# Attention products of few keys made 128 rows deep with zero weights, and three VectorE steps of the first layer's chunks put at the priority of the weight splits

## The chip, the cores and the metric

The kernel runs on one core of one Trainium2 chip. The metric is the device time in microseconds (us), from the first to the last instruction with what lies around them; the median of the runs is compared. Before the change the median of three runs is 934.2 us (933.96 to 939.34). A core has a matrix engine (TensorE, PE in the profile, with its weight loads as PEld), VectorE (DVE), ScalarE (ACT), GpSimd (POOL) and SyncE (SP), which issues most of the DMAs.

## The reference

One inference step of a two-layer decoder, for a prompt of 512 tokens and 8 samples of 4 tokens each (544 columns in all), model width 1024, float32. Cut to what matters here:

```python
def ssd_scan(xdt, adt, bm, cm, init):            # first layer: state-space mixer, chunks of 128 tokens
    seg = exp(where(tri, a_cs[..., :, None] - a_cs[..., None, :], -inf))
    cb = einsum("bctgn,bcsgn->bcgts", Cc, Bc)
    m = einsum("bcgts,bgjcts->bcgjts", cb, seg)                  # masked products times decays
    y_diag = einsum("bcgjts,bcsgjp->bctgjp", m, X)               # X = x * dt
    chunk_states = einsum("bctgn,bgjct,bctgjp->cbgjpn", Bc, decay_in, X)
    ...
def dilated_attn_prompt(q, k, v, bvec, dil, nw): # second layer: keys at distances 0, d, .., nw*d
    p = exp(scores - lse[..., None])
    o = einsum("brnhqk,brnkhd->brnqhd", p, vb)
def dilated_attn_sample(q, kc, vc, bvec, dil, nw, n_old):  # 1024 cached rows and the 4 new ones
    scores = einsum("bthd,btjhd->bthj", q, kg) * (q.shape[-1] ** -0.5) + bvec.T[None, None]
    o = einsum("bthj,btjhd->bthd", p, vg)
```

There are three dilation groups (windows 128, 512, 2048 with distances 1, 4, 16), 8 key heads of width 128, 32 state-space heads in 4 groups. The projections before and after, the norms, the convolution and the shared keys and values complete the step.

## The kernel before, in words

Float32 weights and activations of the big projections are split into a high and a low part (`whi`, `wlo`, `nh`, `nl`, ...), and three products replace one. `split_w` (lines 200 to 211) does this for a weight tile: ScalarE copies the high part (L205), VectorE subtracts it (L206). `load_w` (L213) fetches a tile and puts the split at high priority (`tc.high_priority()`), so that the scheduler places it ahead of waiting work on its engine. The order of the instructions of each engine is otherwise the scheduler's, from the order of the program and its own estimates.

The first layer (about 60 to 350 us of the span) is a filler of input projections (`filler_a`: products into `pa` and `pb`, then the convolution `co` on ScalarE and VectorE, L635 to L646, or the gate `uz`, L681), into which the units of the state-space mixer are woven: for each of 4 groups four chunks of 128 tokens (`ssm_chunk`) and two quads of samples (`ssm_quad`). A chunk on TensorE: transposes and a product into the PSUM tiles `cbp` and `xp`; VectorE then makes `xdt` and `xdd` (`xp` scaled by two vectors, L743 and L745), `cbm` (the masked product, L747) and `m` (L748); on later turns TensorE multiplies into `csp`, `yo` and `yd`. A quad does the like, with `cbs`, `xdt`, `xdd` at high priority already, and updates the states with four products `up` (L855 to L862). These PSUM tiles share five buffers (`pss`), so a product into a new tile can wait until VectorE or ScalarE has read an old one. `xdt` and `xdd` of chunks and quads share three SBUF buffers.

The second layer's attention (about 590 to 870 us) is woven the same way: the filler (`pair_filler`, then `out_proj`) makes the query and gate projections, and 48 units `attend(h, n)` (head h, query block n of 128) and `sample(h, q)` run beside them, each in stages. In `attend` the scores of the two wider groups stand in w = 32 (n + 1) columns for each class of positions modulo 4; the probabilities are transposed (`ptp`), copied by ScalarE into `pt` (L1403, L1404), and multiplied with the values (`pv`): blocks of 128 keys with 128 columns, then for each of the 4 classes a product of w key rows and 32 columns into its own 32 partitions (L1410). In `sample` the transposed probabilities `wt` of 640 cached keys are multiplied with the cached values `vc` into `so`, 5 blocks of 128 keys and 32 columns for each of 4 samples, and then the 4 new keys: a product of 4 key rows (`vn`, L1486). A float32 product appears in the trace as two matmuls with two weight loads. The cached keys `kc` and values `vc` (640 KB a load, two buffers each) come through SP's queue, as do the weights.

The lines that set these products:

```python
        pt = wk.tile([128, 3, 128], F32, name="pt", bufs=2)                       # L1402
        nc.scalar.copy(pt[0:w, 2, :], tp[0:w, 2, :])                              # L1404
        for r in range(4):                                                        # L1410
            mm(pv[32 * r:32 * r + 32, :], pt[0:w, 2, 32 * r:32 * r + 32], vr[0:w, r, :], ...)
...
                    mm(so[rows, :], wt[0:TS, 5, rows], vn[:, j, :], start=False, stop=True, ...)   # L1486
```

## Time and profile before

| | before |
|---|---|
| median of 3 runs | 934.2 us (933.96 to 939.34) |
| profiled execution, its own time | 930.12 us |
| its span | 928.3 us, 21878 instructions |
| VectorE busy | 683.7 us (74%), 1435 instructions |
| ScalarE busy | 489.6 us (53%) |
| GpSimd busy | 163.9 us (18%) |
| DMA | 168.48 MB, mean 182 GB/s |

The profile is of one execution, taken by the hardware. A group in it is named by line, engine, operation and tiles: `L146 PE MATMUL so<-vn,wt 4*32` is a matmul issued at line 146 (the helper `mm`, which all products share) that writes `so` from `vn` and `wt`, with 4 rows and 32 columns of the array in use. A row of the timeline gives start, duration, engine, line, operation and count, and in square brackets how long the engine had stood idle and what ended that. Neighbouring instructions are merged, and matmuls overlap, so a busy TensorE can still lose time between products.

### The profile page before, as it was taken

To read this page: it belongs to the slowest core of one execution; us is meant where nothing else is said; L and a number is where in the kernel's file an instruction comes from. 1 tells how busy PE (TensorE), PEld (TensorE's weight loads), DVE (VectorE), ACT (ScalarE), POOL (GpSimd) and SP (SyncE) were. 2 spreads that over 40 slices of the span, in tenths; PEclk is the share of its full clock that TensorE was granted. 3 is DMA by queue.
4 is the path that set the end of the run, shared out by engine and by line. 5 is a ranking of instruction groups with operands and counts; after the bars stand their busy time and mean duration, and the time that the engine had idled before them with its cause. 6 is when DMAs were issued, how large, how long until landed. Compare 5 with 4: busy or idle time off the path is not lost.

```text
span 928.3 us, 21878 instructions
## 1 busy us (share of the span) xinstructions
PE 912.0 (98%) x8671; PEld 842.9 (91%) x8671; DVE 683.7 (74%) x1435; ACT 489.6 (53%) x1140; POOL 163.9 (18%) x206
## 2 busy tenths in 40 slices
PE   8999999999999999999999999999999999999997
PEld 8989888988788889999999999988888888888997
DVE  6998899989799799555598346866677766777732
ACT  6678655755665655322255213555555555557642
POOL 2030344533433533111011000000000000000021
PEclk9999999999999999999999999999999999999999
DMA  8224365365357432546286555767867877784511
GB/s 296 92 74 158 97 212 188 122 200 159 127 171 233 138 132 96 159 137 209 84 285 204 190 177 181 255 208 250 279 192 250 265 228 255 258 267 144 191 49 49
DMA packets 80573, 168.48 MB, mean 182 GB/s; under 512 B 19990, under 2 KB 37736, under 8 KB 79960
## 3 DMA queue, kind: packets, MB, share of 16 engines
q1 hardware_dynamic: 73784, 154.60, 50.8%
q10 hardware_dynamic: 5616, 9.75, 2.8%
q0 software_dynamic: 1072, 2.74, 1.2%
q8 instruction: 68, 1.11, 0.5%
q14 instruction: 33, 0.27, 0.1%
HBM read 141.14 MB, written 25.93 MB: 180 GB/s over the span
## 4 chain that ended last, share of the span: by engine, by line
PE 82%; DVE 10%; ACT 2%; DMA 2%; issue 2%; POOL 0%; SPq 0%; ACTq 0%; POOLq 0%; DVEq 0%
PE pa L146 33%; PE pb L146 28%; PE sp L146 3%; PE so L146 3%; PE pv L146 2%; PE s L146 2%; DVE wlo L206 2%; DVE co L641 1%; PE yd L146 1%; DVE vl L874 1%; DMA m<-aed 1%; PE w L149 1%; PE ptp L149 1%; PE csp L146 1%; PE xp L149 1%
## 5 line engine op out<-in xcount | busy, mean ns | idle before, releaser
L205 ACT ACTIVATE whi<-wraw 128x1024 fp32r<-128x1024 f32 x69 | 72.9, 1056 | 95.7 <-PE pb L146 53.0
L206 DVE TENSOR_TENSOR wlo<-wraw,whi 128x1024 fp32r<-128x1024 f32 x69 | 88.8, 1287 | 46.9 <-ACT whi L205 46.4
L146 PE MATMUL pa<-bq,whi 128*128 128x272 f32 x512 | 103.1, 296 | 0.0
L146 PE MATMUL pb<-nl,whi 128*128 128x288 f32 x280 | 83.6, 298 | 0.0
L146 PE MATMUL pb<-nh,wlo 128*128 128x288 f32 x280 | 83.1, 297 | 0.0
L146 PE MATMUL pb<-nh,whi 128*128 128x288 f32 x280 | 83.0, 296 | 0.0
L146 PEld LDWEIGHTS pa<-bq,whi 128*128 128x128 f32 x512 | 81.2, 189 | 0.9
L146 PE MATMUL pa<-nh,whi 128*128 128x256 f32 x280 | 80.0, 286 | 0.0
L146 PE MATMUL pa<-nl,whi 128*128 128x256 f32 x280 | 79.7, 285 | 0.0
L146 PE MATMUL pa<-nh,wlo 128*128 128x256 f32 x280 | 79.1, 282 | 0.0
L146 PE MATMUL pb<-bq,whi 128*128 128x272 f32 x384 | 77.2, 296 | 1.2 <-DVE kv L1225 0.8
L146 PE MATMUL pa<-bq,wlo 128*128 128x272 f32 x256 | 74.2, 290 | 0.0
L641 DVE SCALAR_TENSOR_TENSOR co<-cb,cvp,co 128x568 f32<-128x568 f32 x72 | 65.4, 911 | 1.3 <-ACT co L639 0.7
L146 PEld LDWEIGHTS pb<-bq,whi 128*128 128x128 f32 x384 | 60.8, 189 | 2.5 <-DVE kv L1225 1.0
L1284 ACT ACTIVATE whi<-wraw 128x512 fp32r<-128x512 f32 x64 | 40.1, 627 | 36.4 <-PE pb L146 16.6
L146 PEld LDWEIGHTS pb<-nl,whi 128*128 128x128 f32 x280 | 52.5, 188 | 4.4 <-issue 4.4
L146 PE MATMUL pb<-bq,wlo 128*128 128x272 f32 x192 | 55.4, 289 | 0.0
L146 PEld LDWEIGHTS pb<-nh,wlo 128*128 128x128 f32 x280 | 52.7, 188 | 2.2 <-issue 2.2
L146 PEld LDWEIGHTS pa<-nh,whi 128*128 128x128 f32 x280 | 52.8, 189 | 1.9 <-issue 1.9
L146 PEld LDWEIGHTS pa<-nl,whi 128*128 128x128 f32 x280 | 52.7, 188 | 1.4 <-issue 1.4
L146 PEld LDWEIGHTS pa<-nh,wlo 128*128 128x128 f32 x280 | 52.7, 188 | 0.9 <-issue 0.9
L146 PEld LDWEIGHTS pb<-nh,whi 128*128 128x128 f32 x280 | 52.6, 188 | 0.8 <-issue 0.8
(403 smaller groups left out, 2779.7 us busy)
## 6 DMA issues: line engine op xcount, KB each, us to landing
wraw<-w_in SPq DMA_DIRECT2D x40, 512.0 KB
kc<-ck SPq DMA_DIRECT2D x32, 640.0 KB
vc<-cv SPq DMA_DIRECT2D x32, 640.0 KB
wraw<-wb SPq DMA_DIRECT2D x32, 512.0 KB
s<-s SPq DMA_DIRECT2D x32, 256.0 KB
m<-aed SPq DMA_DIRECT2D x16, 512.0 KB
ssmS<-s ACTq DMA_DIRECT2D x32, 256.0 KB
wraw<-w_out SPq DMA_DIRECT2D x16, 512.0 KB
```

Source lines behind the costliest of these rows:

```text
L146: pin(nc.tensor.matmul(*a, **k))
L149: pin(nc.tensor.transpose(*a))
L205: a = nc.scalar.activation(hi, raw, AF.Copy)
L206: b = lo_eng.tensor_tensor(lo, raw, f32(hi), op=ALU.subtract)
L641: nc.vector.scalar_tensor_tensor(o, cb[:, k:k + n], cvp[:, ti, k:k + 1], o, op0=ALU.mult, op1=ALU.add)
L874: nc.vector.scalar_tensor_tensor(v_l[g][:, i, :], v_t[g][:, i, :], gg, f32(v_h[g][:, i, :]), op0=ALU.mult, op1=ALU.subtract)
L1284: nc.scalar.activation(hi, src[p][j], AF.Copy)
```

## The change

Two edits. In the attention the products of few keys are made 128 rows deep. Four single tiles `ptz[n]`, one for each query block, take the transposed probabilities of the wider groups in their first w rows; their other rows are set to zero once by GpSimd, and the product reads all 128 rows, with all 128 rows of `vr`. `wt` and `vn` of the samples become single tiles allocated once; row 4 and on of `vn` and of `wt[:, 5]` are zeroed once, and the product with the new keys reads 128 rows. `pt` shrinks from three to two blocks. In the first layer `xdt`, `xdd` and `cbm` of a chunk are issued at high priority, as the weight splits are.

```diff
         xdt = wk.tile([128, 8, HP], F32, name="xdt", tag="xd", bufs=3)
-        nc.vector.tensor_tensor(xdt, xph, bc(tok[:, c, 1, hs], HP), op=ALU.mult)
         xdd = wk.tile([128, 8, HP], F32, name="xdd", tag="xd", bufs=3)
-        nc.vector.tensor_tensor(xdd, xph, bc(tok[:, c, 2, hs], HP), op=ALU.mult)
         cbm = wk.tile([128, 128], F32, name="cbm")
-        nc.vector.tensor_tensor(cbm, cbp[:, 0:128], tri, op=ALU.mult)
+        with tc.high_priority():
+            nc.vector.tensor_tensor(xdt, xph, bc(tok[:, c, 1, hs], HP), op=ALU.mult)
+            nc.vector.tensor_tensor(xdd, xph, bc(tok[:, c, 2, hs], HP), op=ALU.mult)
+            nc.vector.tensor_tensor(cbm, cbp[:, 0:128], tri, op=ALU.mult)
...
-    for t_ in qpad + [sbt]:
+
+    ptz = [wk.tile([128, 128], F32, name=f"ptz{i}", bufs=1) for i in range(4)]
+    wt = wk.tile([128, 6, 128], F32, name="wt", bufs=1)
+    vn = wk.tile([128, 4, 128], F32, name="vn", bufs=1)
+    for t_ in qpad + [sbt, vn, wt[:, 5, :]] + ptz:
         nc.gpsimd.memset(t_, 0.0)
...
-        pt = wk.tile([128, 3, 128], F32, name="pt", bufs=2)
+        pt = wk.tile([128, 2, 128], F32, name="pt", bufs=2)
         nc.scalar.copy(pt[:, 0:nk, :], tp[:, 0:nk, :])
-        nc.scalar.copy(pt[0:w, 2, :], tp[0:w, 2, :])
+        nc.scalar.copy(ptz[n][0:w, :], tp[0:w, 2, :])
...
-            mm(pv[32 * r:32 * r + 32, :], pt[0:w, 2, 32 * r:32 * r + 32], vr[0:w, r, :],
+            mm(pv[32 * r:32 * r + 32, :], ptz[n][:, 32 * r:32 * r + 32], vr[:, r, :],
                start=False, stop=True, skip_group_check=True)
...
-        vn = wk.tile([TS, 4, 128], F32, name="vn", bufs=1)
-        dma(vn, dap(vnd, h * 128 + 4 * q * TS * ATH * 128, [[ATH * 128, TS], [TS * ATH * 128, 4], [1, 128]]))
+        dma(vn[0:TS], dap(vnd, h * 128 + 4 * q * TS * ATH * 128, [[ATH * 128, TS], [TS * ATH * 128, 4], [1, 128]]))
...
-        wt = wk.tile([128, 6, 128], F32, name="wt", bufs=1)
...
-                if i < 5:
-                    mm(so[rows, :], wt[:, i, rows], vc[j // 2][:, j % 2, i, :], start=i == 0, stop=False, skip_group_check=True)
-                else:
-                    mm(so[rows, :], wt[0:TS, 5, rows], vn[:, j, :], start=False, stop=True, skip_group_check=True)
+                vals = vc[j // 2][:, j % 2, i, :] if i < 5 else vn[:, j, :]
+                mm(so[rows, :], wt[:, i, rows], vals, start=i == 0, stop=i == 5, skip_group_check=True)
```

TensorE's order of products is the same in both kernels, throughout. VectorE's order moves at about a dozen places of the first layer; ScalarE's, GpSimd's and SP's shift by a few rows there. The first place is VectorE's queue late in the third group's first quad and second chunk, before the change (`st` to `v` finish the chunk, `xr` belongs to the quad; `xdt`, `xdd` and `cbm` are of the next chunk, `wlo` is a weight split):

```order
L761 TENSOR_TENSOR st<-csp,st 128x512
L766 TENSOR_TENSOR ea<-yo,ea 128x512
L220 SCALAR_TENSOR_TENSOR xr<-xdd,csts,xr 128x512
L777 TENSOR_TENSOR v<-yd,ea 128x4x128
L743 TENSOR_TENSOR xdt<-xp,tok 128x512
L206 TENSOR_TENSOR wlo<-wraw,whi 128x1024
L745 TENSOR_TENSOR xdd<-xp,tok 128x512
L747 TENSOR_TENSOR cbm<-cbp,csts 128x128
```

The same place on VectorE after it (line numbers are one higher):

```order
L762 TENSOR_TENSOR st<-csp,st 128x512
L220 SCALAR_TENSOR_TENSOR xr<-xdd,csts,xr 128x512
L767 TENSOR_TENSOR ea<-yo,ea 128x512
L778 TENSOR_TENSOR v<-yd,ea 128x4x128
L746 TENSOR_TENSOR xdt<-xp,tok 128x512
L747 TENSOR_TENSOR xdd<-xp,tok 128x512
L206 TENSOR_TENSOR wlo<-wraw,whi 128x1024
L748 TENSOR_TENSOR cbm<-cbp,csts 128x128
```

`xdd` now stands ahead of the split, `cbm` still behind it, and `xr` ahead of `ea`.

The second place is VectorE's queue some 12 us earlier, in the same quad, before (`co` and `CT` are the convolution, `btr` and `cbs` read the quad's `cbp`):

```order
L641 SCALAR_TENSOR_TENSOR co<-cb,cvp,co 128x568
L828 TENSOR_TENSOR xdt<-xp,tok 128x512
L220 SCALAR_TENSOR_TENSOR btr<-cbp,csts,btr 128x128
L822 TENSOR_TENSOR cbs<-cbp,csts 128x16
L644 SCALAR_TENSOR_TENSOR CT<-cb,co 128x512
```

And after:

```order
L641 SCALAR_TENSOR_TENSOR co<-cb,cvp,co 128x568
L220 SCALAR_TENSOR_TENSOR btr<-cbp,csts,btr 128x128
L823 TENSOR_TENSOR cbs<-cbp,csts 128x16
L829 TENSOR_TENSOR xdt<-xp,tok 128x512
L644 SCALAR_TENSOR_TENSOR CT<-cb,co 128x512
```

`btr` and `cbs` moved ahead of `xdt`.

The third place is the like of the second one group earlier (the second group's first quad), on VectorE before:

```order
L828 TENSOR_TENSOR xdt<-xp,tok 128x512
L220 SCALAR_TENSOR_TENSOR btr<-cbp,csts,btr 128x128
L822 TENSOR_TENSOR cbs<-cbp,csts 128x16
L644 SCALAR_TENSOR_TENSOR CT<-cb,co 128x512
L645 SCALAR_TENSOR_TENSOR CT<-cb,co 128x32
```

And after:

```order
L829 TENSOR_TENSOR xdt<-xp,tok 128x512
L644 SCALAR_TENSOR_TENSOR CT<-cb,co 128x512
L645 SCALAR_TENSOR_TENSOR CT<-cb,co 128x32
L220 SCALAR_TENSOR_TENSOR btr<-cbp,csts,btr 128x128
L823 TENSOR_TENSOR cbs<-cbp,csts 128x16
```

Here `btr` and `cbs` moved behind the two parts of `CT`.

## The prediction

> **What bounds the kernel now.** I read the page first, then the stages, then who waits for whom, and last the timeline of the products that the change touches. The page gives the engines' busy time and the chain that ended last:

> ```profile
> PE 912.0 (98%) x8671; PEld 842.9 (91%) x8671; DVE 683.7 (74%) x1435; ACT 489.6 (53%) x1140; POOL 163.9 (18%) x206
> PE 82%; DVE 10%; ACT 2%; DMA 2%; issue 2%; POOL 0%; SPq 0%; ACTq 0%; POOLq 0%; DVEq 0%
> ```

> The same by stages, with start and end, length, then busy us (and instructions) of PE, PEld, DVE, ACT, POOL, and the DMA share before GB/s:

> ```profile
> 60.00:350.00 290.00, 287.59 (x2366) 257.56 (x2366) 260.94 (x408) 182.13 (x449) 115.80 (x125) 1.00 0.49 160
> 590.00:870.00 280.00, 279.25 (x3511) 245.81 (x3509) 201.38 (x618) 156.13 (x420) 4.59 (x16) 1.00 0.71 236
> ```

> TensorE is never idle for long in either stage. In the first layer all its idle time that another engine ended is this:

> ```profile
> PE up L146 <- DVE xdd L745: 1.6, 1, 1.6
> PE yd L146 <- DVE cbs L822: 0.6, 1, 0.6
> PE xp L149 <- DVE xs L644: 0.2, 1, 0.2
> ```

> So VectorE, though busy for 261 of 290 us, costs TensorE some 2.4 us. In the attention the busy number hides losses, because matmuls overlap. They show in the weight loads. TensorE's row of the products with cached values is first, then the loads of the product with the four new keys and of what follows:

> ```profile
> 605.67 1.30 PE L146 MATMUL so<-vc,wt 128*32 128x128 f32 x40
> 606.90 0.15 PEld L146 LDWEIGHTS so<-vn,wt 4*32 4x32 f32 x8 [0.20 <-issue]
> 607.25 0.16 PEld L146 LDWEIGHTS s<-kc,qpad 128*32 128x32 f32 x8 [0.20 <-PE so L146]
> ```

> The loads stand still for 0.20 us when the rows in use go from 128 to 4, and again when they go back. The same stands around products of 64 rows, not around those of 96 or 128:

> ```profile
> 612.49 0.15 PEld L146 LDWEIGHTS pv<-kv,pt 64*32 64x32 f32 x8
> 612.84 0.16 PEld L146 LDWEIGHTS sp<-kv,qp 128*32 128x32 f32 x8 [0.20 <-issue]
> 618.39 0.13 PEld L146 LDWEIGHTS sp<-kv,qp 128*32 128x32 f32 x4
> 629.28 0.16 PEld L146 LDWEIGHTS pv<-kv,pt 128*32 128x32 f32 x8
> 629.53 0.24 PE L146 MATMUL sp<-kv,qp 128*32 128x64 f32 x4
> 869.95 0.19 PEld L146 LDWEIGHTS pa<-yh,wo 128*128 128x128 f32 x1 [0.20 <-issue]
> ```

> The row at 618.39 follows the 96-row product of block 2 and carries no wait; 629.28 is block 3, already 128 rows, which is what the changed kernel issues everywhere.

> **The attention products, part by part.** The number of products, from the rows of the tiles (two matmuls each, four products a unit):

> ```profile
> L146 PEld LDWEIGHTS so<-vc,wt x640: 106/110/111, 605.7 to 854.3; 128*32 128x32 f32 x160
> L146 PEld LDWEIGHTS so<-vn,wt x128: 101/103/104, 606.9 to 854.6; 4*32 4x32 f32 x128
> L146 PE MATMUL pv<-kv,pt x368: 267/275/377, 600.5 to 869.8; 128*128 128x128 f32 x56, 32*32 32x128 f32 x32, 64*32 64x128 f32 x32, 96*32 96x128 f32 x32
> ```

> Samples: 128 / 8 = 16 units. From the start of `so` to the start of the following product is 607.25 - 605.67 = 1.58 us now. The forty matmuls with `vc` go in ten groups of four; the last starts 1.30 - 0.27 = 1.03 after the first, less 0.02 within its group, so nine steps take 1.01 and one step 0.112. With twelve groups alike, the next product starts twelve steps after the first: 1.34. The gain is 0.24 a unit, 16 x 0.24 = 3.8 us.

> Prompt: eight heads, so eight units of each block. After the wait a load and its matmul start together, so block 1 takes 612.84 - 612.49 = 0.35 from its first narrow product to the next, and block 3 takes 629.53 - 629.28 = 0.25. The gain is 0.10 where the rows are 32 or 64 and a product with 32 columns follows: eight units of block 1 and seven of block 0. The last block 0 is followed by the output projection with 128 columns, which waits anyway (869.95), and blocks 2 and 3 gain nothing. The wait ahead of the narrow products stays, since it is there in block 3 too, where 128 columns give way to 32. 15 x 0.10 = 1.5 us. Together 5.3 us on the engine that sets the end.

> What padding adds: a load of 128 rows takes 110 ns against 103, so 128 x 7 ns = 0.9 us if the loads stood in a row, and nothing if they hide behind products, as those of `vc` do: forty loads of 110 ns within 1.03 us. I take nothing, since block 3 with 128 rows shows the step above already. [...]

> Six more GpSimd memsets stand where these stand now:

> ```profile
> 571.17 0.64 POOL L1178 MEMSET sbt<- 128x644 f32 x1
> 570.99 0.69 DVE L1285 TENSOR_TENSOR wlo<-sums,whi 128x512 fp32r<-128x512 f32 x1 [0.81 <-ACT whi L1284]
> ```

> They write 512 + 5 x 128 = 1152 columns, at 0.64 / 644 each 1.1 us, from 571.8 on. The first narrow product comes at 600, VectorE is not slowed beside a memset (0.69), so I cost them at nothing; without that cover it would be 1.1 us. The rest has one answer: ScalarE's copies, the DMA of `vn`, and the buffers keep their size, places and waits (`vn` and `wt` had one buffer before).

> Now what comes late next. TensorE already waits for cached keys twice:

> ```profile
> PEld s L146 <- DMA kc<-ck: 1.3, 2, 0.7
> ```

> Those loads are issued after the previous `so`, behind others in SP's queue, so where they already end the wait, a faster TensorE only waits longer: in each such stretch one `so` and two `pv` gain 0.24 + 0.20 = 0.44, lost again. 2 x 0.44 = 0.9 us; none lost at best, and all 5.3 at worst if every sample came to wait so. The attention keeps 4.4 us.

> **The first layer.** At the 1.6 us wait, VectorE's and TensorE's rows:

> ```profile
> 249.39 0.67 DVE L743 TENSOR_TENSOR xdt<-xp,tok 128x512 f32<-128x512 f32 x1
> 251.26 1.23 DVE L206 TENSOR_TENSOR wlo<-wraw,whi 128x1024 fp32r<-128x1024 f32 x1 [1.19 <-ACT whi L205]
> 252.40 0.68 DVE L745 TENSOR_TENSOR xdd<-xp,tok 128x512 f32<-128x512 f32 x1
> 253.00 0.28 DVE L747 TENSOR_TENSOR cbm<-cbp,csts 128x128 f32<-128x128 f32 x1
> 253.20 0.18 PEld L146 LDWEIGHTS up<-xr,btr 32*128 32x128 f32 x1 [1.93 <-issue]
> 253.23 0.61 PE L146 MATMUL up<-xr,btr 32*128 32x512 f32 x2 [1.65 <-DVE xdd L745]
> ```

> VectorE stood behind a split that waited for ScalarE, with `xdd` queued behind; TensorE's second `up` needed the buffer that `xdd` frees. Now `xdd` goes first. But the third `up` needs the buffer that `cbm` reads, and `cbm` stays behind the split; it comes 0.60 earlier, by the length of `xdd`. So I take 0.6, with bounds of 0 and 1.9, the whole wait. At the second place of the order:

> ```profile
> 238.62 0.68 DVE L828 TENSOR_TENSOR xdt<-xp,tok 128x512 f32<-128x512 f32 x1
> 239.47 0.16 DVE L822 TENSOR_TENSOR cbs<-cbp,csts 128x16 f32<-128x16 f32 x1
> 239.69 1.09 PE L146 MATMUL yd<-m,xdt 128*64 128x128 f32 x16 [0.57 <-DVE cbs L822]
> ```

> `cbs` goes ahead of `xdt`, some 0.6 earlier, and the 0.57 goes. At the third place it goes the other way:

> ```profile
> 167.65 0.16 DVE L822 TENSOR_TENSOR cbs<-cbp,csts 128x16 f32<-128x16 f32 x1
> 167.73 0.89 DVE L644 SCALAR_TENSOR_TENSOR CT<-cb,co 128x512 f32<-128x512 f32 x1
> 168.62 0.33 PE L146 MATMUL yd<-m,xdt 128*64 128x128 f32 x2
> ```

> `cbs` moves behind `CT` (0.89 and its small part of 0.1) and ends at about 168.8, later than `yd` starts; if that `yd` waits for `cbs` as the other did, it loses 0.2 to 0.4. I take 0.25, bounds 0 and 1. Elsewhere `xdt`, `xdd` and `cbm` overtake convolution steps and, at five places, a split. What waits behind is then 0.6 later each time, and the splits have more room than that:

> ```profile
> 222.75 2.38 DVE L206 TENSOR_TENSOR wlo<-wraw,whi 128x1024 fp32r<-128x1024 f32 x1
> 227.59 0.29 PE L146 MATMUL pa<-nh,wlo 128*128 128x256 f32 x1
> ```

> This one, among the latest, ends 2.5 us before its first use. So nothing is charged there. First layer: 0.6 + 0.57 - 0.25 = 0.9 us gained.

> **The sum.** 4.4 + 0.9 = 5.3 us. The profiled execution took 930.12 us (span 928.3), so it would take 924.8. It lies 4.1 under the median of the runs shown, 934.2, and I carry that distance over: 928.9 us.

> **Rivals.** First, the first layer gives all it can: both waits go whole (1.9 + 0.57), the third place costs nothing, and no key load bites. Then 5.3 + 2.5 = 7.8, 926.4 us. For it: TensorE waits for nothing else there. Against it: `cbm` is still behind the split.

> Second, the cached loads take most of the attention's gain. DMA is busy for 0.71 of the stage, and SP issues them late. If half is lost, 5.3 / 2 = 2.7 is left, with nothing net from the first layer: 931.5 us. Against it: only two of 16 samples waited.

> Third, slower: VectorE's queue is held by a step put forward too early. `cbm` waits for a copy by ScalarE:

> ```profile
> 322.90 0.29 DVE L747 TENSOR_TENSOR cbm<-cbp,csts 128x128 f32<-128x128 f32 x1 [1.46 <-ACT btok L740]
> ```

> Here VectorE stood 1.46 us. The change moves `cbm` forward at six places; behind it queue convolution steps, the splits and the reads that free PSUM, and TensorE waits for these once VectorE is 2.5 us behind. If all six stood 1.46 and TensorE bore it, 8.8 would be lost: 934.2 - 4.4 + 8.8 = 938.6 us. It ends above 934.2 from 4.4 us of such waits on. Against it: at those places ScalarE's copy was done before VectorE came to `cbm`, mostly by over a microsecond, and VectorE waited so only twice in the whole layer.

> Fourth, padded loads no longer slip under running products, so that eight loads in a row cost 8 x 0.11 = 0.88 us where now the narrow group takes 0.35 and the wait ahead of it 0.20. Then 31 units (16 and 15) lose 0.33 each, 10.2 us: 944.4 us. [...]

> Fifth, the waits belong to something else than the rows and stay: 934.2 less 0.9, about 933.3. The missing wait behind 96 rows speaks against it.

> **How the numbers follow.** Chances: forecast 0.55, first rival 0.15, second 0.14, third 0.08, fourth 0.02, fifth 0.04, and 0.02 for a gain beyond all of these. The forecast's own range, with its unknown costs (0 to 0.9 from the key loads, 0 to 1.9 and 0 to 1 from the first layer), is 926.5 to 930.5. Down to the first rival with 1.9 us for the runs' own scatter, and up past the second by 1 us, it holds over 8 in 10: 924.5 to 932.5. A measurement of this kernel can tell about 1% from no change, here below 924.9 or above 943.5. Faster than that needs the first rival and scatter, 0.08; slower needs the third at its worst or the fourth, 0.04; the rest, 0.88, lies within 1%.

> **What would show it.** In the profile after: the loads of `so<-vn` with 128*32 and without a wait, those of `s` behind `so` without one; 0.25 us instead of 0.35 behind `pv` in blocks 0 and 1; longer waits of `s` for `kc`, but at two to four samples only; no wait of `up` for `xdd`, a shorter one for `cbm`; none of `yd` for `cbs` at 239, a small one at 168. The prediction is wrong if TensorE shows new waits in the first layer that add up to over 2 us, if waits for `kc` exceed 2.5 us, or if the 0.20 us waits stand beside 128 rows.

## The result and the profile after

| | before | after |
|---|---|---|
| median of 7 runs, the same rounds | 934.33 us (933.96 to 939.34) | 927.23 us (924.51 to 932.11) |
| ratio, with its 95% interval | | 0.9913 (0.9884 to 0.9941) |
| a second timing, later: 5 runs of after, 23 of before | 933.46 us | 927.1 us, ratio 0.9935 (0.9922 to 0.9948) |
| profiled execution, its own time | 930.12 us | 932.11 us |

The change makes the kernel 6 to 8 us faster, 0.65 to 0.87%, less than the 1% that I counted as telling. The forecast was 928.9 us with a range of 924.5 to 932.5. One thing has to be kept in mind in reading the two profiles: the profiled execution of the changed kernel was the slowest of its seven, and the first one of the kernel before faster than all seven of its timed runs. Side by side they say "2 us slower". Only stage by stage do they say what happened.

First the page's busy times and chain, then the stretches 60 to 350 and 590 to 870 us, of the changed kernel:

```profile
PE 908.9 (98%) x8671; PEld 847.9 (91%) x8671; DVE 687.5 (74%) x1435; ACT 489.9 (53%) x1140; POOL 163.0 (18%) x212
PE 82%; DVE 9%; DMA 4%; ACT 2%; issue 2%; POOL 0%; SPq 0%; POOLq 0%; DVEq 0%; ACTq 0%
```

```profile
60.00:350.00 290.00, 284.75 (x2322) 254.96 (x2321) 259.65 (x399) 179.06 (x446) 114.11 (x125) 0.99 0.48 157
590.00:870.00 280.00, 277.54 (x3548) 252.63 (x3548) 204.58 (x628) 159.06 (x423) 4.59 (x16) 1.00 0.73 243
```

In the 290 us of the first layer TensorE gets through 44 products fewer (2322 for 2366); in the 280 us of the attention through 37 more (3548 for 3511), though it starts late into them. The chain has 4% of waits for transfers where it had 2%. TensorE's order of products is the same in both, so the starts can be compared product by product. From the product that starts at 60.1 us before the change to the one at 360.1, the changed kernel takes 5.6 us longer in this execution; from 360.1 to 572.5 exactly as long; from 572.5 to 873.1, the attention, 3.9 us less.

The loads around the products of few keys, in the changed kernel, a sample and then a prompt block 0:

```profile
611.28 1.03 PEld L146 LDWEIGHTS so<-vc,wt 128*32 128x32 f32 x40 [0.20 <-DMA bt<-bvd]
612.29 0.24 PEld L146 LDWEIGHTS so<-vn,wt 128*32 128x32 f32 x8
612.51 0.24 PEld L146 LDWEIGHTS s<-kc,qpad 128*32 128x32 f32 x8
...
606.52 0.16 PEld L146 LDWEIGHTS pv<-kv,ptz 128*32 128x32 f32 x8
606.66 0.40 PEld L146 LDWEIGHTS sp<-kv,qp 128*32 128x32 f32 x16
```

The waits of 0.20 us ahead of `so<-vn` and of `s` are gone, and that ahead of `sp` behind block 0 (the prediction shows the same rows before the change, for block 1). What TensorE waited for between 60 and 350 us:

```profile
PE xp L149 <- DVE xs L644: 2.1, 1, 2.1
PE up L146 <- DVE cbm L748: 1.4, 1, 1.4
PE yd L146 <- ACT yos L825: 1.2, 1, 1.2
PE pa L146 <- DVE uz L681: 0.5, 1, 0.5
```

The waits for `xdd` and `cbs` that stood there before, 2.2 us, are gone, and 5.2 us of others stand in their place.

### The profile page after: what moved, and what is told of

Read it like the earlier page. It is cut to its first block, busy times and chain, and to the rows that moved or that the text cites. A ratio compares the mean times of both kernels' runs of the same rounds, so it can differ in the third digit from the quotient of the medians.

```text
span 930.2 us, 21888 instructions
## 1 busy us (share of the span) xinstructions
PE 908.9 (98%) x8671; PEld 847.9 (91%) x8671; DVE 687.5 (74%) x1435; ACT 489.9 (53%) x1140; POOL 163.0 (18%) x212
## 4 chain that ended last, share of the span: by engine, by line
PE 82%; DVE 9%; DMA 4%; ACT 2%; issue 2%; POOL 0%; SPq 0%; POOLq 0%; DVEq 0%; ACTq 0%
PE pa L146 33%; PE pb L146 28%; PE sp L146 3%; PE pv L146 2%; PE so L146 2%; PE s L146 2%; DVE wlo L206 2%; DMA kc<-ck 1%; PE yd L146 1%; DMA m<-aed 1%; DVE co L641 1%; PE csp L146 1%; PE w L149 1%; PE ptp L149 1%; PE xp L149 1%
## 5 line engine op out<-in xcount | busy, mean ns | idle before, releaser
L205 ACT ACTIVATE whi<-wraw 128x1024 fp32r<-128x1024 f32 x69 | 72.8, 1056 | 97.0 <-PE pb L146 57.2
L206 DVE TENSOR_TENSOR wlo<-wraw,whi 128x1024 fp32r<-128x1024 f32 x69 | 89.6, 1298 | 45.1 <-ACT whi L205 44.7
L146 PE MATMUL pa<-bq,whi 128*128 128x272 f32 x512 | 103.1, 296 | 0.0
L146 PE MATMUL pb<-nl,whi 128*128 128x288 f32 x280 | 84.0, 300 | 0.0
L146 PE MATMUL pb<-nh,wlo 128*128 128x288 f32 x280 | 83.5, 298 | 0.0
L146 PE MATMUL pb<-nh,whi 128*128 128x288 f32 x280 | 83.4, 298 | 0.0
L146 PEld LDWEIGHTS pa<-bq,whi 128*128 128x128 f32 x512 | 81.2, 189 | 0.9
L146 PE MATMUL pa<-nh,whi 128*128 128x256 f32 x280 | 81.1, 290 | 0.5 <-DVE uz L681 0.5
L146 PE MATMUL pa<-nl,whi 128*128 128x256 f32 x280 | 80.7, 288 | 0.0
L146 PE MATMUL pa<-nh,wlo 128*128 128x256 f32 x280 | 80.1, 286 | 0.0
L146 PE MATMUL pb<-bq,whi 128*128 128x272 f32 x384 | 77.2, 296 | 1.3 <-DVE kv L1230 1.1
L146 PE MATMUL pa<-bq,wlo 128*128 128x272 f32 x256 | 74.2, 290 | 0.0
L146 PEld LDWEIGHTS pb<-bq,whi 128*128 128x128 f32 x384 | 60.8, 189 | 2.6 <-DVE kv L1230 1.3
L146 PEld LDWEIGHTS pb<-nl,whi 128*128 128x128 f32 x280 | 53.0, 189 | 4.4 <-issue 4.4
L146 PEld LDWEIGHTS pa<-nh,whi 128*128 128x128 f32 x280 | 53.8, 192 | 2.6 <-issue 1.9
L146 PE MATMUL pb<-bq,wlo 128*128 128x272 f32 x192 | 55.5, 289 | 0.0
L146 PEld LDWEIGHTS pa<-nl,whi 128*128 128x128 f32 x280 | 53.8, 192 | 1.4 <-issue 1.4
L146 PEld LDWEIGHTS pb<-nh,wlo 128*128 128x128 f32 x280 | 53.1, 190 | 2.2 <-issue 2.2
L146 PEld LDWEIGHTS pa<-nh,wlo 128*128 128x128 f32 x280 | 53.8, 192 | 0.9 <-issue 0.9
L146 PEld LDWEIGHTS pb<-nh,whi 128*128 128x128 f32 x280 | 53.0, 189 | 0.8 <-issue 0.8
```

The lines of the kernel that those rows point to most:

```text
L146: pin(nc.tensor.matmul(*a, **k))
L205: a = nc.scalar.activation(hi, raw, AF.Copy)
L206: b = lo_eng.tensor_tensor(lo, raw, f32(hi), op=ALU.subtract)
```

## Experiments

### The two edits apart, and both kernels again

The first two kernels each have one half of the diff shown above, the whole of it for that half; the other two are the kernels before and after, unchanged, for a second trace. All four were timed in the same rounds.

> Attention edit alone; the first layer is issued as in the kernel before. By my sum the attention keeps 4.4 us of its 5.3: 929.9 us beside a kernel before of 934.3. If the whole measured gain of 7.1 us came from the attention, 927.2; if the cached loads took half of it, 931.6. In the trace the time from the start of so to the next product is 1.34 us instead of 1.58 in every one of the 16 samples, 0.24 instead of 0.35 in blocks 0 and 1 of the prompt.

> First-layer edit alone; the attention as in the kernel before. By my sum 0.9 us faster: 933.4 us. If both waits went whole and nothing took their place (first rival), 2.5 faster: 931.8. If the measured 7.1 less the 3.95 of the attention in the profiled execution is the first layer's, 3.1 faster: 931.2. If the new waits of the profiled execution of the changed kernel (for xs 1.9 us more, for yos 1.2, for uz 0.5, cbm in place of xdd, and two stretches of the clock at 0.66 with 1.5 us each) are the rule, 3 to 6 slower: 937 to 940.

> The kernel before again, for a second trace of it. Its one trace (930.1 us) lies 4 us under the median of its timed runs. If those runs lose time in the first layer that the one trace does not show (a longer wait, a stretch at a lower clock), this trace shows it, near 934, and the gain of the first layer's edit is larger than the one trace let see; if the trace comes out near 930 again with no such loss, the distance lies outside the profile's reach.

> The changed kernel again, for a second trace of it, in the same rounds as the other three. If edits add up, its gain is the sum of those of the two single edits, near 7 us (927.2). In the trace: the attention gains 4 us again; the first layer's waits for xs (2.1 us) and yos (1.2 us) come again if VectorE's order causes them, and do not if the arrival of a transfer did; the clock's two stretches at 0.66 come only behind waits of over 1.3 us.

| | median | ratio to before | its trace: first layer | its trace: attention |
|---|---|---|---|---|
| before (23 runs; the trace is the second one) | 933.46 us | | +4.4 us | +0.2 us |
| attention edit alone | 928.13 | 0.9932 (0.9918 to 0.9947) | +0.3 | -6.0 |
| first-layer edit alone | 934.36 | 0.9998 (0.9985 to 1.0012) | +3.1 | 0.0 |
| both | 927.10 | 0.9935 (0.9922 to 0.9948) | +1.2 | -4.3 |

The last two columns are against the first trace of before, from the same three products as above. The whole gain is the attention's: 4.9 to 7.7 us by the interval. The first layer's edit lies between 1.4 us faster and 1.1 slower by its interval; no effect at all and the 0.9 us that I had forecast both lie in it. Both together give no more than the one alone.

The second trace of before explains why its first one was faster than its timed runs. TensorE's waits in the first layer there, and the stretches around the longest of them (length, busy us and instructions of PE, PEld, DVE, ACT and POOL, granted clock, DMA share, GB/s):

```profile
PE up L146 <- DVE xdd L745: 2.4, 1, 2.4
PE xp L149 <- DVE xs L644: 0.9, 1, 0.9
PE yd L146 <- DVE cbs L822: 0.6, 1, 0.6
```

```profile
252.00:256.00 4.00, 1.66 (x22) 1.15 (x21) 2.04 (x4) 3.86 (x13) 0.00 (x0) 0.86 0.22 66
256.00:260.00 4.00, 3.92 (x15) 3.52 (x16) 4.00 (x8) 2.86 (x7) 0.00 (x0) 0.50 0.37 131
```

The same wait for `xdd` that took 1.65 us in the first trace takes 2.4 here, and behind it TensorE's granted clock falls to 0.50. The wait and its consequence cost 3.2 us more than in the first trace (by the starts of the products from 252 to 272 us), where by the starts the wait itself costs 2.1. So the place that I priced at "0.6, at most 1.9" was worth some 5 us in that execution (2.1 and 3.2). The second trace is 5.9 us longer than the first in all: 4.4 in the first layer, 0.2 in the attention, and 1.3 ahead of 60 us, where TensorE's clock fell too:

```profile
50.04:53.45 3.41, 3.41 (x17) 3.41 (x18) 2.97 (x9) 2.47 (x5) 0.26 (x1) 0.50 0.00 0
```

That place lies ahead of both edits, and nine of the fourteen traces have such a stretch there, with and without the edits.

In the second trace of the changed kernel TensorE waits, in the first layer, for `yos` and `uz` as in the first (1.2 and 0.5 us), and for:

```profile
PE xp L149 <- DVE xs L644: 1.6, 2, 1.3
```

The waits of `yd` for `yos` and of `pa` for `uz` come in all three traces with the edit (that of the first-layer edit alone is the third), at the same size. They belong to the order. That for `xs` changes its size and place, and that for `cbm` its size, down to nothing.

### Which chunk of the first layer does what

High priority was put in force for single chunks, the attention edit always with it (chunks and groups counted from 0 in the code; line numbers in these kernels are one higher than in the changed one):

```diff
-        with tc.high_priority():
+        with tc.high_priority() if (g, c) == (2, 2) else contextlib.nullcontext():
```

and in its place `(g, c) != (1, 1)`, `(g, c) == (1, 1)` and `(g, c) in ((2, 1), (2, 2))`. Each chunk moves its own places on VectorE and leaves the others, so these can be read one by one.

> The attention edit, and of the first layer's edit only the third chunk of the third group, which moves xdd ahead of one split on VectorE and nothing else on any engine. Theory of the places: the wait of the second up (1.5 to 2.4 us in the traces without the edit) goes, and the stretch of lower clock that follows it in some executions with it; what is left of a wait of the third up for cbm is 0 to 1.4. Beside the attention edit alone (928.1 us) 1 to 4 us faster, 925.5. Theory of chance (the waits shift with the arrival of transfers, and no single place matters): 928.1 within 1 us.

> The changed kernel without high priority in the second chunk of the second group, the one that moves btr and cbs behind CT at the third place and three convolution steps around. Theory of the places: the waits of yd for yos (1.2 us) and of pa for uz (0.5) near 169 and 175 are gone, that of xs at about 210 falls below 1 us, and the rest of the gains stays: 2 to 4 us faster than the changed kernel (927.1), 924.5. Theory of chance: 927.1 within 1 us, and the waits for yos and uz are still there or stand elsewhere.

> The attention edit, and of the first layer's edit only the second chunk of the second group. Theory of the places: TensorE waits 1.2 us for yos near 169 and 0.5 for uz near 175, and up to 2 us for xs near 210, while the waits of yd for cbs and of up for xdd near 239 and 251 stay: 2 to 4 us slower than the attention edit alone (928.1), 931. Theory of chance: 928.1 within 1 us.

> The attention edit, and of the first layer's edit the second and the third chunk of the third group. Theory of the places: as with the third chunk alone, and the 0.57 us wait of yd for cbs near 239 is gone too: 0.6 us faster than that one, 925. Theory of chance: 928.1 within 1 us.

| first layer's edit on | median | ratio to before | its trace: first layer |
|---|---|---|---|
| no chunk (above) | 928.13 us | 0.9932 (0.9918 to 0.9947) | +0.3 us |
| third group's third chunk | 927.44 | 0.9925 (0.9900 to 0.9950) | +0.3 |
| third group's second and third | 925.63 | 0.9902 (0.9878 to 0.9926) | -1.6 |
| all but second group's second | 925.16 | 0.9896 (0.9870 to 0.9921) | -2.2 |
| second group's second alone | 932.40 | 0.9976 (0.9959 to 0.9993) | +6.3 |
| all chunks (above) | 927.10 | 0.9935 (0.9922 to 0.9948) | +1.2 |

The theory of the places holds for the second group's second chunk: alone it costs 0.0044 of 934, some 4 us, with its interval clear of that of no chunk. All the others together gain: 0.9896 in this timing, whose interval still touches that of no chunk, and 0.9891 (0.9868 to 0.9914) in a second one, which does not. The third group's third chunk alone came out where the theory of chance had put it (927.44, for 928.1 within 1 us), and not at 925.5. Its trace says why: by the starts of the products the second `up` gains 2.14 us there, and the third loses 1.91 again, in a wait for `cbm`. TensorE's waits with the harmful chunk alone:

```profile
PE up L147 <- DVE xdd L748: 2.1, 1, 2.1
PE yd L147 <- ACT yos L826: 1.2, 1, 1.2
...
PE pa L147 <- DVE uz L682: 0.5, 1, 0.5
PE up L147 <- DVE cbm L749: 0.4, 1, 0.4
...
```

and without it all that is left in the layer is

```profile
PE up L147 <- DVE cbm L749: 0.4, 1, 0.4
PE xp L150 <- DVE xs L645: 0.2, 1, 0.2
```

How it costs is seen on ScalarE, at the third place of the prediction. Before the change (first trace):

```profile
166.96 0.68 ACT L643 ACTIVATE cb<-co 128x568 f32<-128x568 f32 x1 [1.49 <-DVE co L641]
...
168.62 1.09 PE L146 MATMUL yd<-m,xdt 128*64 128x128 f32 x16
168.67 0.57 ACT L824 COPY yos<-yos 128x512 f32<-128x512 f32 x1
```

and after it (second trace of the changed kernel):

```profile
166.38 1.92 DVE L641 SCALAR_TENSOR_TENSOR co<-cb,cvp,co 128x568 f32<-128x568 f32 x1
...
168.33 0.68 ACT L643 ACTIVATE cb<-co 128x568 f32<-128x568 f32 x1 [1.05 <-DVE co L641]
...
169.21 0.56 ACT L825 COPY yos<-yos 128x512 f32<-128x512 f32 x1
...
169.83 0.77 PE L146 MATMUL yd<-m,xdt 128*64 128x128 f32 x10 [1.16 <-ACT yos L825]
...
171.61 0.16 DVE L823 TENSOR_TENSOR cbs<-cbp,csts 128x16 f32<-128x16 f32 x1
```

In that chunk `xdd` goes ahead of convolution steps, and ScalarE's step on the last of those starts 1.4 us later (168.33 for 166.96). The copy of `yos` stands behind it on ScalarE, and `yd` waits for that copy. Before the change it did not: it starts at 168.62, ahead of the copy. This can be read in the two programs' waits on TensorE, row by row, of the kernel before:

```
1042 L146 MATMUL csp<-xdd,btok 128x512 [waits DVE_49,Activation_49]
1044 L146 MATMUL yd<-m,xdt 64x128 [waits DVE_49]
```

and of the changed one:

```
1042 L146 MATMUL csp<-xdd,btok 128x512 [waits DVE_49]
1043 L146 MATMUL yo<-CT,st 128x128 [waits Activation_49]
1045 L146 MATMUL yd<-m,xdt 64x128 [waits Activation_49]
```

The products stand in the same order, but they wait for another engine. The built programs name the buffers: of the five shared ones `yd` has that of `yos` in the changed kernel, which the copy frees, and before the change that of the quad's `cbp`, which `btr` and `cbs` read. The kernel with that chunk alone has the buffers and waits of the changed kernel here, the one without it those of before. Of the 1.2 us some 0.6 is the new wait itself (before the change the copy ended at 168.67 + 0.57 = 169.24, 0.6 after the start of `yd`), and 0.5 is the copy's later start (169.21 for 168.67). `cbs`, which I had watched, runs at 171.61, after `yd` has started: nothing there waits for it.

The wait for `cbm` was 1.5 us with the third chunk alone, and none with the second and third. The second chunk puts `xr`, which `up` reads, ahead of `ea`; I have not taken that apart further. Nor is it settled why the single chunk costs 4 us where its own waits come to 2.8 by the starts of the products (1.2 for `yos`, 0.7 around `uz`, and 0.9 where the third `up` waits for `cbm` at 182 us, which no other trace has). Its trace has the clock's fall behind the 2.1 us wait for `xdd` too, but the kernel before has that wait as well: the mean granted clock is 0.995 in the runs of both, and 0.997 in those of the three other kernels of the table that were timed beside them and no longer wait for `xdd`.

### Does the number of rows fall in two classes?

Two kernels with the attention edit alone, reading fewer rows:

```diff
-            mm(pv[...], ptz[n][:, 32 * r:32 * r + 32], vr[:, r, :], ...)
+            mm(pv[...], ptz[n][0:max(w, 96), 32 * r:32 * r + 32], vr[0:max(w, 96), r, :], ...)
...
-                vals = vc[j // 2][:, j % 2, i, :] if i < 5 else vn[:, j, :]
-                mm(so[rows, :], wt[:, i, rows], vals, ...)
+                nr = 128 if i < 5 else 64
+                vals = vc[j // 2][:, j % 2, i, :] if i < 5 else vn[0:nr, j, :]
+                mm(so[rows, :], wt[0:nr, i, rows], vals, ...)
```

and the same with 64 in the first place and 96 in the second.

> Attention edit with fewer rows: the products with the new keys read 64 rows instead of 4 or 128, those of the prompt's blocks 0 and 1 read 96 instead of 32 and 64 or 128. My theory, that the number of rows in use falls in two classes (up to 64, and from 96 on) and only a change of class costs: so to the next product 1.58 us as before the change, since 64 rows are another class than 128; the prompt's blocks 0.243 as with 128 rows. Rival, that the cost shrinks evenly with the rows that are left out: so 1.45, blocks 0 and 1 at 0.27. Rival, that only exactly 128 rows are free of it: so 1.58, blocks 0.35.

> The other way round: 96 rows for the new keys, 64 for the prompt's blocks 0 and 1. Theory of two classes: so to the next product 1.34 us as with 128 rows; the prompt's blocks 0.35 as before the change. Rival of an even cost: so 1.40, blocks 0.30. Rival of exactly 128: so 1.58, blocks 0.35.

Loads of the first kernel (64 rows for the new keys, 96 for the blocks):

```profile
602.87 0.16 PEld L146 LDWEIGHTS pv<-kv,ptz 96*32 96x32 f32 x8
603.00 0.74 PEld L146 LDWEIGHTS sp<-kv,qp 128*32 128x32 f32 x17
...
608.86 0.15 PEld L146 LDWEIGHTS so<-vn,wt 64*32 64x32 f32 x8 [0.20 <-issue]
609.21 0.16 PEld L146 LDWEIGHTS s<-kc,qpad 128*32 128x32 f32 x8 [0.20 <-PE so L146]
```

and of the second (96 and 64):

```profile
604.31 0.15 PEld L146 LDWEIGHTS pv<-kv,ptz 64*32 64x32 f32 x8
604.67 0.32 PEld L146 LDWEIGHTS sp<-kv,qp 128*32 128x32 f32 x16 [0.20 <-issue]
...
610.21 0.24 PEld L146 LDWEIGHTS so<-vn,wt 96*32 96x32 f32 x8
610.43 0.24 PEld L146 LDWEIGHTS s<-kc,qpad 128*32 128x32 f32 x8
```

By the starts of the products, `so` to the next one takes 1.58 us with 64 rows and 1.34 with 96; the blocks 0.352 with 64 and 0.243 with 96. So 4, 32 and 64 rows cost beside 128 (1.58 us with 4 rows too, and 0.20 us of wait behind the 32 rows of block 0 before the change), and 96 rows do not; nothing shrinks evenly here. Other products of the kernel before, with 128 columns, narrow the border: a load of 66 rows and the one of 128 rows behind it carry no wait, and no more do the other changes between 66 and 128 rows in that trace, 37 in all:

```profile
396.51 0.19 PEld L146 LDWEIGHTS bvp<-oh,relt 66*128 66x128 f32 x1
396.64 0.19 PEld L146 LDWEIGHTS pa<-vh,whi 128*128 128x128 f32 x1
```

Whether 4, 32 and 64 rows are one class among themselves is not shown: no run puts them side by side. In the first layer the loads behind the 32 rows of `up`, with 128 columns as well, stand still for 0.24 us, 16 times; whether zeros would pay there was not tried.

### What of the attention's gain the loads of cached keys take

> The kernel without the second group's second chunk (925.2 us), with the loads of cached keys issued by GpSimd instead of SyncE, where they stand behind loads of values, biases and weights that wait for buffers of their own. If the waits of s for kc (1.3 to 3.4 us in the traces so far) come from their place in SyncE's queue, the loads are issued as soon as their buffers are free, the waits go, and the kernel gains 1 to 2.5 us: 923.5. If they come from the buffers, which the sample before frees, or from the transfers' own speed, nothing changes: 925.2 within 1. If GpSimd's queue is the slower one, s waits longer at many samples: 928 and more.

> The changed kernel without the second group's second chunk once more, beside the last one and on the same chip: 925.2 us again within 1 if the first timing was no accident; its trace has waits of s for kc of 1.3 to 3.4 us and no wait of yd for yos.

```diff
-            dma(kc[jp], ck[h, q, :, 2 * jp:2 * jp + 2, :])
+            nc.gpsimd.dma_start(kc[jp], ck[h, q, :, 2 * jp:2 * jp + 2, :])
```

The kernel without the harmful chunk came to 924.51 us and 0.9891 (0.9868 to 0.9914), as before. With the loads on GpSimd's queue it came to 931.32 and 0.9957 (0.9940 to 0.9974), 0.0066 or 6 us slower. The loads of `s` now wait for `kc` once, 1.7 us, where they waited twice, 2.0 us. In TensorE's waits from 572 us on others stand ahead of it:

```profile
PE pb L147 <- DVE qp L1222: 1.7, 3, 0.9
PE w L150 <- ACT ss L1466: 1.5, 1, 1.5
...
PE s L147 <- DMA kc<-ck: 0.8, 1, 0.8
...
```

None of my three answers was right. VectorE's order, which the scheduler drew up anew for the loads on the other queue, moved at 90 places, and the attention, which gains 5.8 us in the trace of the kernel without the harmful chunk beside it, gains nothing in this one: the waits that the new order brought take it all. So it stays open what a freer queue for these loads would be worth.

What the loads take is seen without it. Eight traces have the whole attention edit. Their attention stage gains, against the first trace of before, 6.0, 5.8, 5.1, 4.4, 4.3, 3.9, 3.3 and 2.8 us, a mean of 4.5; the weight loads of `s` wait for `kc` in them, in the same order, 1.5, 2.0, 2.5, 2.8, 3.4, 2.8, 4.0 and 4.0 us. The row for the first, the attention edit alone, for the changed kernel's profiled execution, and for the last, the kernel without the harmful chunk:

```profile
PEld s L146 <- DMA kc<-ck: 1.5, 2, 1.2
```

```profile
PEld s L146 <- DMA kc<-ck: 2.8, 3, 1.3
```

```profile
PEld s L147 <- DMA kc<-ck: 4.0, 3, 2.0
```

By pairs of products the edit's gain before this loss is the same in all eight, 6.0 us; how much is lost depends mostly on when a few loads arrive.

## Why the prediction was right, and where it was not

The total (928.9 for a measured 927.2) and the sign were right. The attention's step was right in kind and nearly in size. The first layer's was wrong at one place out of three, and its error and the attention's went opposite ways (in the timed runs of the single edits the attention gains 6.3 for 4.4, the first layer 0.2 for 0.9), so it is in part luck that the total came so near.

**Samples, 3.8 us forecast.** Measured 3.9, by pairs of products in the trace of the attention edit alone: 1.81 at the sixteen steps from `so<-vc` to `so<-vn`, 1.73 behind `so<-vn`, 0.39 within it. Start to next product is 1.335 us in every sample, for 1.34 forecast.

**Prompt blocks, 1.5 us.** Measured 1.64. Another 0.41 came between the `sp` products behind the blocks, which I had not looked at: the first of them no longer starts late. So the edit gives 6.0 us, for 5.3 in my sum.

**Padding and memsets at nothing.** Right: the loads of 128 rows take 110 ns for 103 and lie within running products (eight loads of `so<-vn` within 0.24 us), as those of `vc` did (forty loads, 26 ns apart). At the memsets no product comes late. The rival of padded loads that no longer overlap fell with that.

**Cached keys, 0.9 us.** The right mechanism, somewhat too small: the mean gain of 4.5 for 6.0 says that 1.5 is lost, and single executions lose 0 to 3.2. Of the 1.5 some 0.3 is not the keys': it went into a wait of `pb` for `kv` late in the stage, 1.1 us for 0.8, which the faster TensorE reaches sooner; that I had not listed. So the keys take about 1.2. I took two samples as bitten, and the trace shows two to four; the one at 693 us in the second trace, for instance, had not waited before. The attention keeps 4.5 on the mean of the eight traces, and 6.0 in that of the attention edit alone, whose timed runs say 4.9 to 7.7; 4.4 was forecast.

**The wait for `xdd`, 0.6 us, bounds 0 and 1.9.** The mechanism was as told (`xdd` passes the split, `cbm` may be late next), and the third `up` did wait for `cbm`, 0 to 1.5 us in the traces. But the price was wrong in two ways. By the starts of the products the second `up` gains 2.14 us in all three traces with the whole edit, more than the bound, and the third gives 0, 0.6 and 1.8 of it back: 0.6 stands for net gains of 2.1, 1.5 and 0.3. And the wait had been longer than in the execution I saw in three of the six traces that have it (1.8, 2.1 and 2.4 us for 1.65), in two of them with a stretch at a lower clock behind it. The bound of 1.9 came from one execution.

**The wait for `cbs`, 0.57 us.** Right: 0.64 less in all three traces.

**The third place, a loss of 0.25 us, bounds 0 and 1.** This is the step that failed. I priced the one row that the quoted order showed moving, `cbs`, and assumed that `yd` would wait for it as at the second place. It waits for ScalarE's copy of `yos` instead, since it has taken that tile's buffer. The same chunk moved `xdd` ahead of convolution steps; I had counted those overtakings among "the splits have more room than that", and the room of the splits says nothing about ScalarE, which waits for the convolution with that copy behind it. I had compared only the order of TensorE's products, which is the same, and not what they wait for, which isn't. It cost 1.2 us for `yos` and 0.7 around `uz` in all three traces, and that chunk alone makes 4 us of difference in the timing. It is a relative of my third rival (a step put forward too early holds a queue, others stand behind it), but on ScalarE's queue and at one place, not by `cbm` on VectorE's at six.

By the prediction's own signs the first layer's part was refuted by the first profile after the change: 5.2 us of new waits, where over 2 was to mean wrong. A second sign struck too: `s` waits 2.8 us for `kc` there and 3.4 in the second trace, where over 2.5 was to mean wrong. The total still came out because the same edit takes away a wait that in half of the traces with it costs more than in the first one, so that by the timed runs the layer ends up even within its interval. Of the 4.1 us between the first profiled execution and the median, which I carried over unexplained, the second trace explains the kind: longer waits at the same places, and stretches at a lower clock there and ahead of 60 us.

**A faster version.** With the second group's second chunk left out of the first layer's edit, the kernel took 925.16 and 924.51 us in two timings, ratios 0.9896 (0.9870 to 0.9921) and 0.9891 (0.9868 to 0.9914): some 10 us under before. Against the second timing of the changed kernel (0.9922 to 0.9948) that is faster; against the first (0.9884 to 0.9941) the intervals overlap.

## What to carry to other kernels

Where a row of matmuls changes between few and many rows of contraction, look at the weight loads, not at TensorE's busy share: here a stall of 0.20 us stood there between 4, 32 or 64 rows and 128, and zeros in the unused rows took it away, with the deeper loads (110 ns for 103) still hidden. What was won is less than the stall: 0.11 to 0.12 us for each change, by the starts of the products. Where an edit raises the priority of steps, follow what they overtake to the next engine's queue, compare the waits and the buffers of the products as well as their order, and do so chunk by chunk: one placing can lose what all the others gain. And a wait priced from one execution has its size from that one; look for it in a second before bounding it.

## What was not expected of the hardware

```profile
215.66:219.07 3.41, 3.41 (x18) 3.41 (x17) 3.41 (x6) 3.00 (x8) 0.00 (x0) 0.50 0.38 91
```

```profile
214.30 0.33 PE L149 MATMUL xp<-ident,xs 128*128 128x128 f32 x1 [2.14 <-DVE xs L644]
...
215.30 0.28 PE L146 MATMUL pa<-nl,whi 128*128 128x256 f32 x1
215.42 0.28 PE L146 MATMUL pa<-nh,wlo 128*128 128x256 f32 x1
...
215.86 0.41 PE L146 MATMUL pa<-nh,wlo 128*128 128x256 f32 x1
216.07 0.41 PE L146 MATMUL pa<-nh,whi 128*128 128x256 f32 x1
...
219.10 0.30 PE L146 MATMUL pb<-nh,wlo 128*128 128x288 f32 x1
219.24 0.29 PE L146 MATMUL pb<-nh,whi 128*128 128x288 f32 x1
```

From 1.4 us after the wait on, products start 0.21 us apart where they stood 0.12 apart, and from 219.1 on 0.14 again (`pb` has more columns). By the starts of the products that costs 1.5 us on top of the wait. In the fourteen traces, all four waits of 2.1 us and more in the first layer were followed by such a stretch, and of the eight of 1.3 to 1.8 us one was; once it came behind a wait of only 0.6, among products of few columns. In the changed kernel's profiled execution a wait of 2.2 us for `whi`, at 8 us and so ahead of the layer, had none behind it: the clock is 1.00 there up to 215.66. Ahead of 60 us all fourteen traces have the same wait of 1.4 to 1.5 us, for `x`, and behind it the clock fell in nine. So the wait of 2.4 us in the second trace of before, on the engine that sets the end, cost twice its length (some 5 us, where the clock stayed low for 6.83 us), and whether such a stretch follows a wait differs between executions. In the traces these stretches last 3.41 us or twice that, the clock is 0.50 in them and 1.00 between them, and they lie whole multiples of 3.41 us apart: in the changed kernel's profiled execution the second one starts at 260.03, thirteen times 3.41 behind the one at 215.66, and the 40.96 us between them are at 1.00. Counted from the kernel's first instruction this rhythm stands elsewhere from trace to trace: 215.66 is 0.6 us past a multiple of 3.413, and the 50.04 of the second trace of before 2.3 us. What decides whether a stretch follows one of the shorter waits was not tried.
